# Each matmul of 512 moving columns made as two of 256, in the products with results by token, in a decoder layer on one core

## The chip, the core and the metric

The kernel runs on one core of one Trainium2 chip. The metric is the time of one execution on the device, in microseconds; the median of the timed runs counts. A profile of one execution shows what each engine did: PE is TensorE's matmul, PEld its load of a stationary tile, DVE is VectorE, ACT is ScalarE, POOL is GpSimd, SP is SyncE, which issues the DMAs.

## What is computed

One hybrid decoder layer for 256 tokens of 2048 features, in float32: a SwiGLU half-step, a mixer of two branches (MLA attention and HGRN2), and a second SwiGLU half-step, each with a norm ahead and one behind.

```python
D_MODEL, SEQ, D_FF, IN_COLS = 2048, 256, 5632, 13376

def swiglu(h, w_gate, w_up, w_down):
    return (jax.nn.silu(h @ w_gate) * (h @ w_up)) @ w_down
...
def token_mixer(h, positions, w_in, ...):
    proj = h @ w_in
    c_q, c_kv, k_rope, hq, hf, hi, hg, gate_a, gate_b = split_columns(proj)
    y_a = mla_branch(c_q, c_kv, k_rope, positions, ...)
    y_b = hgrn2_branch(hq, hf, hi, hg, lower_bound, ...)
    merged = jax.nn.sigmoid(gate_a) * y_a + jax.nn.sigmoid(gate_b) * y_b
    return merged @ w_out
...
        x = x + 0.5 * rmsnorm(swiglu(rmsnorm(x, ...), ...), ffn1_norm_post)
        x = x + rmsnorm(token_mixer(rmsnorm(x, ...), ...), mix_norm_post)
        x = x + 0.5 * rmsnorm(swiglu(rmsnorm(x, ...), ...), ffn2_norm_post)
```

Nearly all of the work is products of the 256 tokens with weight matrices, which are read once from memory.

## The kernel before

**Operands.** Every float32 operand of a large product is held as an exact sum of two parts of type float32r, `hi` and `lo`. A product is the sum of three: hi·hi, hi·lo and lo·hi. The activations stand transposed in SBUF as `[128 features, part, k-tile, 256 tokens]` (`h`, `after`, `h2` for the normed input of a stage; `at` for the SwiGLU's inner values; `mg` for the merged branches; `cqT`, `ckvT` for the two latents). Weights arrive by DMA on SP's queue in tiles `raw` of 128 x 1024 (512 KB, four buffers, line 83). ACT casts such a tile to its `hi` part `whi` (line 95), DVE subtracts to get `wlo` (line 96), with four buffers each. Where a tile has to be kept for later, both parts go into one tile `wpair` of a stage's own pool.

**Two kinds of product.** `gemm_t` (lines 111 to 115) holds weights as the stationary operand, 128 columns of them, and moves the tokens: the result is transposed, [column, token]. There `hi` weights move 512 columns (256 tokens in both parts) and `lo` weights 256. `gemm_n` holds the activations, 128 tokens at a time, as the stationary operand and moves the weights: the result is [token, column], one PSUM bank of 512 columns for each half of the tokens. It calls `_tok` for each k-tile and each half `tt` of the tokens; `_tok` makes the three matmuls of lines 126, 127 and 128 (hi·hi, hi·lo, lo·hi), the first two with the same stationary tile. A weight tile of 1024 holds two k-tiles of 512 columns, so it feeds twelve matmuls. A call with n=256 (the attention's values, `w_v`) has four k-tiles of 256 columns in a weight tile, and 24 matmuls.

**Where `gemm_n` is used.** With 512 columns: four products for the down projection of each half-step (stationary `at`, 44 k-tiles), the first gate and up columns of each half-step (`h`), the latents `c_q` and `c_kv`, the values and gates of the HGRN branch (`after`), the rotary part of the queries (`cqT`, four k-tiles) and four products for `w_out` (`mg`). With 256 columns: the eight products of `w_v` (`ckvT`, four k-tiles).

**Late halves.** At the end of a stage the last product (`closing`) lets the first half of the tokens finish its last `late` k-tiles before the second half starts them, so that the norm and residual of the first half run beside the second half's matmuls. The weights of those k-tiles are held, the first three tiles in `whi`/`wlo`, the others in `wpair`. The first products of the next stage do the same with all their k-tiles.

**Order.** Engines run their queues in order. The queues are filled by a scheduler in the order of the program; a block under `ahead()` is put ahead by 400 instructions (`AHEAD`), which is how a stage's closing chain (norm, transposes' results) gets in front of the weight casts.

Of the kernel before, what the change touches and what calls it, by code (L numbers as in the profile page):

```python
# [19 lines left out]
P = 128  # L20
# [16 lines left out]

# Where the next operand's transposes stand in program order, along the product that runs beside them (see gemm_n), and
# by how many instructions the rest of that operand's chain is put ahead; columns of the residual at a time.
AHEAD = 400  # L40
# [8 lines left out]
def _two_pi_parts():  # L49
    """2 pi as a sum of four 12-bit numbers and a rest."""  # L50
    parts, rest = [], TWO_PI
    for _ in range(4):
        step = 2.0 ** (np.floor(np.log2(rest)) - 11)
        c = np.floor(rest / step) * step
        parts.append(float(c))
        rest -= c
    parts.append(float(np.float32(rest)))
    return parts


class Ops:
    """Pools and the pieces that the stages share."""

# [15 lines left out]

# [1 line left out]
    def fetch(self, src):  # L81
# [17 lines left out]
    def gemm_t(self, w, act, kt):  # L99
        """256 weight columns, result transposed: a bank for 128 columns, [column, token] in two addends."""  # L100
        nc = self.nc
        ps = self.mm.tile([P, 2, 512], F32, name="mm")
        for g in range(kt // 4):
            hi, lo = self.load_w(w[g])
            for i in range(4):
                k = g * 4 + i
                for j in range(2):
                    c = slice(i * 256 + j * P, i * 256 + (j + 1) * P)
                    both = act(k)
                    if k == 0:  # L110
                        nc.tensor.matmul(ps[:, j], hi[:, c], both, start=True, stop=False)  # L111
                        nc.tensor.matmul(ps[:, j, 0:T], lo[:, c], both[:, 0], start=False, stop=False)  # L112
                    else:
                        nc.tensor.matmul(ps[:, j, 0:T], lo[:, c], both[:, 0], start=False, stop=False)  # L114
                        nc.tensor.matmul(ps[:, j], hi[:, c], both, start=False, stop=k == kt - 1)  # L115
        return ps

    def total(self, out, ps):
        """The sum of gemm_t's two addends."""
        self.nc.scalar.copy(out=out, in_=ps[:, :, T:512])  # L120
        self.nc.vector.tensor_tensor(out=out, in0=out, in1=ps[:, :, 0:T], op=ALU.add)

    def _tok(self, ps, hi, lo, act, k, kt, i, n, tt):
        nc = self.nc
        r, c, both, o = slice(tt * P, (tt + 1) * P), slice(i * n, (i + 1) * n), act(k), ps[tt][:, 0:n]
        nc.tensor.matmul(o, both[:, 0, r], hi[:, c], start=k == 0, stop=False)  # L126
        nc.tensor.matmul(o, both[:, 0, r], lo[:, c], start=False, stop=False)  # L127
        nc.tensor.matmul(o, both[:, 1, r], hi[:, c], start=False, stop=k == kt - 1)  # L128

    def gemm_n(self, w, act, kt, n=512, late=0, pool=None, own=0, hooks=()):  # L130
        """n weight columns, result [token, column], a bank for each half of the tokens.

        The first half of the tokens ends its last `late` k-tiles before the second half starts them. Their
        weights are in `pool`, but for the first `own` tiles. `hooks` are functions to call at points that run
        from -1 to 0 along the first half of the tokens, and from 0 to 1 along the second's last k-tiles."""
        kg = 1024 // n
# [29 lines left out]

# [1 line left out]
    def square_sum(self, acc, src):  # L168
# [3 lines left out]
    def rstd_of(self, ssq, n, width, half=False):  # L172
        """ssq [P, n] sums of squares -> 1 / sqrt(mean + eps), or half of it."""
        f = 4.0 if half else 1.0
# [19 lines left out]
    def transposed(self, src, act, c, tt):  # L194
        """split(transpose(src)) into the k-tiles 4c.. of act."""
        pt = self.tp.tile([P, 4, P], F32, name="tp")
# [9 lines left out]
    def prenorm(self, x, ssq, wname, act, tt, ws=None):  # L206
        """act = split(transpose(x * rstd * w)) for half of the tokens."""
        with self.ahead():
# [9 lines left out]
    def weighted(self, ps, c, z, wname):  # L218
        """z = y * w, a quarter of the columns."""
        w = self.bcast(wname, c)  # L220
        self.nc.vector.tensor_tensor(out=z[:, c * 512:(c + 1) * 512], in0=ps, in1=w, op=ALU.mult)

    def residual(self, x, z, rstd, done):
        """x += rstd * z, some of the columns at a time."""
        for c in range(D // RC):
# [4 lines left out]

    def closing(self, w, act, kt, late, own, pool, post, half, x_src, x_dst, nxt):
        """The last product of a stage, its norm, the residual, and the next stage's operand.

        Returns the hooks of the next product, which end the operand."""
        z = [pool.tile([P, D], F32, name=f"z{tt}") for tt in range(NT)]
# [32 lines left out]
def layer_kernel(ctx, tc, a, out):  # L268
# [9 lines left out]
    def ffn(n, act, fp, x_src, x_dst, nxt, hooks=()):  # L278
        at = [fp.tile([P, 2, 4, T], F32R, name="at", tag="s8", bufs=ops.slots) for _ in range(KF // 4)]
        wg, wu = a[f"ffn{n}_w_gate"], a[f"ffn{n}_w_up"]  # L280

        # the first columns by halves of the tokens
        pg = ops.gemm_n(a[f"ffn{n}_w_gate0"], act, KD, late=KD, pool=fp, own=4, hooks=hooks)
# [26 lines left out]

# [1 line left out]
    with fpool(1) as fp:  # L312
# [20 lines left out]

# [1 line left out]
    mix = ExitStack()  # L335
# [48 lines left out]

# [1 line left out]
    ops.slots = KF // 4  # L386
# [4 lines left out]
def rope_tables(ops, pool):  # L391
    """cos and sin of positions * inv_freq as [token, half of the tokens, HALF]."""
    nc, a = ops.nc, ops.a
# [15 lines left out]

    # whole turns off: their number in parts of ten bits, so that each product with a part of 2 pi is exact  # L410
    turns = pool.tile([P, n], F32, name="turns")
# [21 lines left out]
def mla(ops, mp, c_q, hm, h, oa, gate):  # L433
# [16 lines left out]
    def rope(dst, src, tt, n):  # L450
        """src [P, n, 64] -> dst, rotated."""
        s1, s2 = src[:, :, 0:HALF], src[:, :, HALF:ROPE]
# [16 lines left out]

    # k_rope: product transposed, back to [token, dim], rotated, transposed, for the even and the odd  # L470
    # head of a pair in its half of the partitions, with zeros in the other
    hi, lo = ops.load_w(a["w_krope"][0])
# [51 lines left out]
    def scores(pair, qn, kn, v):  # L524
        """The weights of a pair of heads, and what is left to do with them."""
        ws = []
# [44 lines left out]

    # a pair's projections, the weights of the pair before, and the output of that one later on
    later = []
# [25 lines left out]
def hgrn(ops, gp, h, ob, fill):  # L599
# [7 lines left out]

    # lower bound: first row of the softmax over the two rows of logits
    lg = gp.tile([P, 2, NH], F32, name="lg")
# [13 lines left out]
    def pair_in(pr, step):  # L623
        """q, f, k as [feature, half of the tokens, head, token]; the second half runs back in time."""
        tmp = lambda: gp.tile([P, 2, 2, P], F32, name="tmp", bufs=2)
# [27 lines left out]
    def values_in(g):  # L653
        """Values of four heads, [token, half of the tokens, head and feature]."""
        ps = ops.gemm_n(a["w_hi"][g], h, KD)
# [4 lines left out]
    def gates_in(g):  # L660
        """Their output gates, with the norm's weights."""
        ps = ops.gemm_n(a["w_hg"][g], h, KD)
# [10 lines left out]
    def scan(pr, q, f, k, four):  # L673
        """pre: products of f within blocks up to and with t; suf: products after s to the end of the block.

        Scores of pairs (s, t) in the two halves of a block of 2n tokens are k suf . q pre with blocks of n. In
        the second half of the tokens time runs back, so that there an earlier s has the place of a later
        one in the first half: one product gives both."""
        pre = f
# [6 lines left out]
        def part(t, n, early):  # L686
            """The earlier (or later) halves of the blocks of 2n: [P, half of the tokens, block, n]."""
            a0, a1 = (0, n) if early else (n, 0)
            return view(t, a0, [[256 + a1 - a0, 2], [2 * n, 128 // n], [1, n]])

        def ends(t, n, early):
            """The last element in time of those halves, over n columns."""
            a0, a1 = (n - 1, n) if early else (2 * n - 1, 0)
            return view(t, a0, [[256 + a1 - a0, 2], [2 * n, 128 // n], [0, n]])

        def halves(t, n, tt, early):
            """The same as part, of one half of the tokens: [P, block, n]."""
            off = n if early == bool(tt) else 0
# [91 lines left out]

    # a pair's products, the scores of the one before, and the output of the one before that
    later = []
# [30 lines left out]

# [1 line left out]
def _tiles(w, cols, group):  # L825
    """[K, C] -> [C / cols, K / (group * 128), 128, group * cols]"""
    k, c = w.shape
# [5 lines left out]
def _tokens(x):  # L833
    """Tokens in the kernel's order: the second half runs back in time."""
    return np.concatenate([x[:P], x[P:][::-1]])
# [63 lines left out]
```

## Time and profile before

| | |
|---|---|
| median of three timed runs | 2564.39 us (2564.30 to 2566.51) |
| profiled execution, first to last instruction (span) | 2564.2 us; no other time of it is listed, so 0.2 us lies between it and the median |
| PE busy | 2521.4 us, 98% |
| PEld busy (runs beside PE) | 2147.1 us |
| DVE, ACT, POOL busy | 1477.7, 1186.9, 181.1 us |
| granted TensorE clock, mean | 0.999 |
| moved from and to memory | 481 MB, 188 GB/s |
| under lines 126, 127, 128: matmuls of 512 columns | 1,296 each, 3,888 in all |
| under the same lines: matmuls of 256 columns (`w_v`) | 64 each, 192 in all |

In the profile's rows `L126 PE MATMUL mm<-whi,at 128*128 128x512` is a matmul of line 126 that writes `mm`, moves 512 columns of `whi` and has a stationary tile of `at` of 128 x 128. The duration of one matmul includes its way through the array; consecutive ones overlap, so that the time from start to start is less than the duration. In the timeline a row starts with the start in us from the start of the span and the duration in us.

### The profile page before, as it was taken

The numbers are of one execution on the slowest core, as the hardware profiler recorded it, in microseconds if no ns is written. First come the engines' busy times: TensorE is split into PE (matmuls) and PEld (weight loads), VectorE is DVE, ScalarE is ACT, GpSimd is POOL, SyncE is SP. The second block draws the span as 40 slices with busy tenths as digits, with TensorE's granted clock in tenths as the row PEclk, the third lists the DMA queues.
The fourth block names the chain that finished last, engine by engine and source line by source line (L and its number), as shares of the span: only waits on it lengthen the run. The fifth ranks groups of instructions, "written<-read, shape, count | busy, mean of one in ns | idle before, by whom it ended". The sixth has DMA issues, their size and how long they took to land.

```text
span 2564.2 us, 33907 instructions
## 1 busy us (share of the span) xinstructions
PE 2521.4 (98%) x13316; PEld 2147.1 (84%) x13316; DVE 1477.7 (58%) x1732; ACT 1186.9 (46%) x1552; POOL 181.1 (7%) x181
## 2 busy tenths in 40 slices
PE   8999999999999999999999999999999999999998
PEld 6888888888878898888888888888788888888887
DVE  5555555544466666556777776555655555554444
ACT  5444444434344556444444444444544444443433
POOL 0000000000000100111323231120000000000000
PEclk9999999999999999999999999999999999999999
DMA  7555555556686444555545444567755555555655
GB/s 255 174 188 189 188 183 190 188 188 199 201 271 188 162 140 148 188 181 181 165 163 169 161 157 158 188 205 242 231 175 188 187 186 188 189 189 188 197 195 184
DMA packets 137248, 481.13 MB, mean 188 GB/s; under 512 B 15616, under 2 KB 16000, under 8 KB 136320
## 3 DMA queue, kind: packets, MB, share of 16 engines
q1 hardware_dynamic: 137088, 478.97, 57.3%
q8 instruction: 104, 1.70, 0.3%
q14 instruction: 56, 0.46, 0.1%
HBM read 472.61 MB, written 6.29 MB: 187 GB/s over the span
## 4 chain that ended last, share of the span: by engine, by line
PE 93%; DVE 3%; POOL 1%; issue 1%; DMA 1%; ACT 1%; SPq 0%; POOLq 0%; DVEq 0%; ACTq 0%
PE mm L115 34%; PE mm L114 18%; PE mm L126 11%; PE mm L127 11%; PE mm L128 11%; PE mm L111 2%; PE mm L112 1%; POOL suf L706 1%; PE tp L198 0%; DVE sT L711 0%; PE sp L534 0%; PE sp L533 0%; DVE wlo L96 0%; PE sp L728 0%; PE tp L565 0%
## 5 line engine op out<-in xcount | busy, mean ns | idle before, releaser
L96 DVE TENSOR_TENSOR wlo<-raw,whi 128x1024 fp32r<-128x1024 f32 x826 | 1024.8, 1243 | 763.5 <-ACT whi L95 762.3
L95 ACT CAST whi<-raw 128x1024 fp32r<-128x1024 f32 x826 | 865.7, 1050 | 891.2 <-PE mm L115 425.3
L115 PE MATMUL mm<-h,whi 128*128 128x512 f32 x2400 | 846.0, 393 | 0.0
L114 PE MATMUL mm<-h,wlo 128*128 128x256 f32 x2400 | 678.1, 283 | 0.0
L115 PEld LDWEIGHTS mm<-h,whi 128*128 128x128 f32 x2400 | 450.7, 188 | 100.7
L114 PEld LDWEIGHTS mm<-h,wlo 128*128 128x128 f32 x2400 | 451.2, 188 | 3.8
L115 PE MATMUL mm<-after,whi 128*128 128x512 f32 x960 | 340.1, 394 | 0.0
L114 PE MATMUL mm<-after,wlo 128*128 128x256 f32 x960 | 273.1, 284 | 0.0
L127 PE MATMUL mm<-wlo,at 128*128 128x512 f32 x664 | 262.0, 395 | 0.0
L126 PE MATMUL mm<-whi,at 128*128 128x512 f32 x664 | 262.0, 395 | 0.0
L128 PE MATMUL mm<-whi,at 128*128 128x512 f32 x664 | 261.7, 395 | 0.0
L115 PEld LDWEIGHTS mm<-after,whi 128*128 128x128 f32 x960 | 180.4, 188 | 38.9
L114 PEld LDWEIGHTS mm<-after,wlo 128*128 128x128 f32 x960 | 180.6, 188 | 1.2
L126 PEld LDWEIGHTS mm<-whi,at 128*128 128x128 f32 x664 | 125.1, 188 | 29.2
L128 PEld LDWEIGHTS mm<-whi,at 128*128 128x128 f32 x664 | 125.1, 188 | 29.2
L127 PEld LDWEIGHTS mm<-wlo,at 128*128 128x128 f32 x664 | 125.1, 188 | 29.2
L178 POOL TENSOR_TENSOR rs<-ms,mhalf 128x1 f32<-128x1 f32 x16 | 9.7, 605 | 1633.3 <-DVE ms L176 1633.3
L126 PE MATMUL mm<-whi,after 128*128 128x512 f32 x304 | 120.9, 398 | 1.2 <-ACT after L164 1.2
L128 PE MATMUL mm<-whi,after 128*128 128x512 f32 x304 | 120.1, 395 | 0.0
L127 PE MATMUL mm<-wlo,after 128*128 128x512 f32 x304 | 120.0, 395 | 0.0
L115 PE MATMUL mm<-oa,whi 128*128 128x512 f32 x240 | 84.6, 393 | 0.0
L115 PE MATMUL mm<-ob,whi 128*128 128x512 f32 x240 | 84.6, 393 | 0.0
(276 smaller groups left out, 2860.9 us busy)
## 6 DMA issues: line engine op xcount, KB each, us to landing
raw<-in_ffn_w_gate SPq DMA_DIRECT2D x176, 512.0 KB, 4.3
raw<-in_ffn_w_up SPq DMA_DIRECT2D x176, 512.0 KB, 3.5
raw<-in_ffn_w_down SPq DMA_DIRECT2D x176, 512.0 KB, 4.3
raw<-in_w_ga SPq DMA_DIRECT2D x32, 512.0 KB, 3.4
raw<-in_mla_w_o SPq DMA_DIRECT2D x32, 512.0 KB, 3.6
raw<-in_w_hq SPq DMA_DIRECT2D x32, 512.0 KB, 3.6
raw<-in_w_hf SPq DMA_DIRECT2D x32, 512.0 KB, 3.5
raw<-in_w_hi SPq DMA_DIRECT2D x32, 512.0 KB, 3.5
```

Of the source, the lines that this page charges most:

```text
L95: nc.scalar.copy(out=hi, in_=raw)
L96: nc.vector.tensor_tensor(out=lo, in0=raw, in1=hi.bitcast(F32), op=ALU.subtract)
L111: nc.tensor.matmul(ps[:, j], hi[:, c], both, start=True, stop=False)
L112: nc.tensor.matmul(ps[:, j, 0:T], lo[:, c], both[:, 0], start=False, stop=False)
L114: nc.tensor.matmul(ps[:, j, 0:T], lo[:, c], both[:, 0], start=False, stop=False)
L115: nc.tensor.matmul(ps[:, j], hi[:, c], both, start=False, stop=k == kt - 1)
L126: nc.tensor.matmul(o, both[:, 0, r], hi[:, c], start=k == 0, stop=False)
L127: nc.tensor.matmul(o, both[:, 0, r], lo[:, c], start=False, stop=False)
L128: nc.tensor.matmul(o, both[:, 1, r], hi[:, c], start=False, stop=k == kt - 1)
L178: self.nc.gpsimd.tensor_tensor(out=r, in0=ms, in1=self.mhalf[:, 0:n], op=ALU.pow)
L706: G.tensor_tensor(out=part(suf, n, True), in0=part(suf, n, True), in1=ends(pre, n, False), op=ALU.mult)
```

## The change

In `_tok`, each matmul over n moving columns becomes one for every 256 of them, with the same stationary tile, into the two halves of the same PSUM bank. The very first matmul of an accumulation (k-tile 0, hi·hi), which clears the bank, stays whole. Calls with n=256 stay as they were. Comments and docstrings are dropped; nothing else differs in the source. From line 129 on, line numbers are four higher.

```diff
         r, c, both, o = slice(tt * P, (tt + 1) * P), slice(i * n, (i + 1) * n), act(k), ps[tt][:, 0:n]
-        nc.tensor.matmul(o, both[:, 0, r], hi[:, c], start=k == 0, stop=False)
-        nc.tensor.matmul(o, both[:, 0, r], lo[:, c], start=False, stop=False)
-        nc.tensor.matmul(o, both[:, 1, r], hi[:, c], start=False, stop=k == kt - 1)
+        for part, w in ((0, hi), (0, lo), (1, hi)):
+            if k == 0 and w is hi and part == 0:
+                nc.tensor.matmul(o, both[:, part, r], w[:, c], start=True, stop=False)
+                continue
+            for b in range(0, n, 256):
+                nc.tensor.matmul(o[:, b:b + 256], both[:, part, r], w[:, i * n + b:i * n + b + 256], start=False,
+                                 stop=k == kt - 1 and part == 1 and b + 256 == n)
```

On TensorE, at the start of the first down product, behind the last transposed product of the gate and up columns (`h`). Before:

```order
L115 MATMUL mm<-h_86,whi 128x512
L126 MATMUL mm<-whi,at 128x512
L127 MATMUL mm<-wlo,at 128x512
L128 MATMUL mm<-whi,at 128x512
L126 MATMUL mm<-whi,at 128x512
L127 MATMUL mm<-wlo,at 128x512
L128 MATMUL mm<-whi,at 128x512
L126 MATMUL mm<-whi,at 128x512
```

And now:

```order
L115 MATMUL mm<-h_86,whi 128x512
L128 MATMUL mm<-whi,at 128x512
L131 MATMUL mm<-wlo,at 128x256 x2
L131 MATMUL mm<-whi,at 128x256 x2
L128 MATMUL mm<-whi,at 128x512
L131 MATMUL mm<-wlo,at 128x256 x2
L131 MATMUL mm<-whi,at 128x256 x4
L131 MATMUL mm<-wlo,at 128x256 x2
```

The six matmuls of k-tile 0 (two halves of the tokens) become ten; from k-tile 1 on each matmul stands twice, and the order of the three products is kept.

The scheduler's lead of 400 instructions now spans fewer k-tiles, so a few neighbouring rows of ACT, DVE and SP change places. On ACT, around the third and the start of the fourth product of `w_out` (`ssq` rows are the squares of that product's result, which let its bank go). Before:

```order
L95 CAST whi<-raw 128x1024 x6
L95 CAST wpair<-raw 128x1024
L95 CAST whi<-raw 128x1024
L95 CAST wpair<-raw 128x1024
L170 ACTIVATE junk,ssq_14529<-mm 128x512
L95 CAST wpair<-raw 128x1024
L170 ACTIVATE junk,ssq_14530<-mm 128x512
L95 CAST wpair<-raw 128x1024 x2
```

And now:

```order
L95 CAST whi<-raw 128x1024 x5
L95 CAST wpair<-raw 128x1024
L95 CAST whi<-raw 128x1024
L95 CAST wpair<-raw 128x1024
L95 CAST whi<-raw 128x1024
L95 CAST wpair<-raw 128x1024
L174 ACTIVATE junk,ssq_16749<-mm 128x512
L95 CAST wpair<-raw 128x1024
L174 ACTIVATE junk,ssq_16750<-mm 128x512
L95 CAST wpair<-raw 128x1024
```

One more cast of held weights stands ahead of the first square.

## The prediction

> **What bounds the kernel now.** I read the page first (busy shares, chain, groups), then the stretches by engine, then the timeline of TensorE's rows. From the page:
>
> ```profile
> span 2564.2 us, 33907 instructions
> PE 2521.4 (98%) x13316; PEld 2147.1 (84%) x13316; DVE 1477.7 (58%) x1732; ACT 1186.9 (46%) x1552; POOL 181.1 (7%) x181
> PE 93%; DVE 3%; POOL 1%; issue 1%; DMA 1%; ACT 1%; SPq 0%; POOLq 0%; DVEq 0%; ACTq 0%
> PE mm L115 34%; PE mm L114 18%; PE mm L126 11%; PE mm L127 11%; PE mm L128 11%; PE mm L111 2%; PE mm L112 1%; POOL suf L706 1%; PE tp L198 0%; DVE sT L711 0%; PE sp L534 0%; PE sp L533 0%; DVE wlo L96 0%; PE sp L728 0%; PE tp L565 0%
> L96 DVE TENSOR_TENSOR wlo<-raw,whi 128x1024 fp32r<-128x1024 f32 x826 | 1024.8, 1243 | 763.5 <-ACT whi L95 762.3
> L95 ACT CAST whi<-raw 128x1024 fp32r<-128x1024 f32 x826 | 865.7, 1050 | 891.2 <-PE mm L115 425.3
> ```
>
> TensorE is busy for 98% of the span and is 93% of the chain that ended last. The three lines that the change rewrites, L126 to L128, are 11% each: a third of the chain. The engines that prepare weights are far from full: a tile of 1024 weight columns costs ACT 1.05 us and DVE 1.24 us and feeds twelve matmuls of 512 columns, which take 2.8 us (below). So whatever changes the time between the starts of these matmuls, which I call the pitch, moves the end of the program by the same amount.
>
> The mean of one matmul in the groups (395 ns) is no pitch: consecutive matmuls overlap, so I take starts from the timeline. In the down product of the first half-step, the first and the last of 57 matmuls in a row:
>
> ```profile
> 639.77 0.39 PE L127 MATMUL mm<-wlo,at 128*128 128x512 f32 x1
> ...
> 652.78 0.39 PE L126 MATMUL mm<-whi,at 128*128 128x512 f32 x1
> ```
>
> 56 steps in 13.01 us: 232.3 ns for 512 columns. The other two kinds of stretch under these lines are the output product of the mixer (first and last of 7), and weights held in the pool of their own, `wpair` (first and last of 16):
>
> ```profile
> 1774.62 0.39 PE L126 MATMUL mm<-whi,mg 128*128 128x512 f32 x1
> ...
> 1776.02 0.39 PE L126 MATMUL mm<-whi,mg 128*128 128x512 f32 x1
> 742.46 0.39 PE L128 MATMUL mm<-wpair,at 128*128 128x512 f32 x1
> ...
> 745.86 0.39 PE L128 MATMUL mm<-wpair,at 128*128 128x512 f32 x1
> ```
>
> 6 steps in 1.40 us, 233.3 ns; 15 steps in 3.40 us, 226.7 ns. The same instruction thus has two paces, 226.7 and some 232 to 233 ns, with nothing waiting in either.
>
> **The change part by part.** The built program has 13,060 matmul instructions before and 16,892 after. The 3,832 more are 3,832 of the 3,888 matmuls of 512 columns, each now two; the 56 that open an accumulation stay whole. The profile's line counts give the split by kind (three lines of each): 420 move `wpair`, 316 are whole-tile matmuls on `mg`, the remaining 3,096 are like the `at` row. Each new matmul brings a weight load of its own: the profile has as many loads as matmuls, and L126 and L127, which use one stationary tile after the other, each have theirs.
>
> The two costs to find are therefore the pitch of a matmul of 256 columns and whether its load hides. The product for the attention's values runs through the very same lines with 256 columns (n=256), on the same `whi` and `wlo` buffers. Its eight products are the nearest row in form:
>
> ```profile
> 897.62 0.36 PE L126 MATMUL mm<-whi,ckvT 128*128 128x256 f32 x1
> 897.83 0.28 PE L127 MATMUL mm<-wlo,ckvT 128*128 128x256 f32 x1
> 897.94 0.28 PE L128 MATMUL mm<-whi,ckvT 128*128 128x256 f32 x1
> 898.06 0.28 PE L126 MATMUL mm<-whi,ckvT 128*128 128x256 f32 x1
> 898.18 0.28 PE L127 MATMUL mm<-wlo,ckvT 128*128 128x256 f32 x1
> 898.30 0.28 PE L128 MATMUL mm<-whi,ckvT 128*128 128x256 f32 x1
> ...
> 900.23 0.28 PE L127 MATMUL mm<-wlo,ckvT 128*128 128x256 f32 x1
> 847.25 0.28 PE L126 MATMUL mm<-whi,ckvT 128*128 128x256 f32 x1
> 847.25 0.19 PEld L127 LDWEIGHTS mm<-wlo,ckvT 128*128 128x128 f32 x1
> 847.36 0.28 PE L127 MATMUL mm<-wlo,ckvT 128*128 128x256 f32 x1
> 847.37 0.19 PEld L128 LDWEIGHTS mm<-whi,ckvT 128*128 128x128 f32 x1
> ```
>
> After some uneven steps of 0.11 to 0.12 us, 17 steps take 1.93 us: 113.5 ns, so two halves take 227.0 ns. The last four rows show the loads (PEld): each starts with the matmul ahead of it and lasts 0.19 us, and the next matmul still starts 0.11 us later. Loads of consecutive matmuls overlap each other and the matmuls; the added 3,832 loads cost nothing by themselves at this pitch. The cover is the matmul ahead; without it a load of 0.19 us would stand alone.
>
> The Trainium skill has a rule against the change: its page "TensorE: Matmul & The Clock Gate", Part 3, section "The mechanism", says that a weight load overlaps matmuls in flight only when it targets another row group. All loads here fill all 128 rows, so by that rule 3,832 added loads of 0.19 us would be exposed, some 728 us; the trace's rows above contradict it, and I give it no chance.
>
> Two other rows bound the pitch from above. The product for the rotary key has 256 moving columns and stationary tiles of 64 columns (first and last of 15):
>
> ```profile
> 813.37 0.28 PE L477 MATMUL mm<-after,whi 128*64 128x256 f32 x1
> ...
> 815.01 0.28 PE L479 MATMUL mm<-after,wlo 128*64 128x256 f32 x1
> 300.02 0.40 PE L115 MATMUL mm<-h,whi 128*128 128x512 f32 x1
> 300.25 0.28 PE L114 MATMUL mm<-h,wlo 128*128 128x256 f32 x1
> 300.37 0.39 PE L115 MATMUL mm<-h,whi 128*128 128x512 f32 x1
> ```
>
> 14 steps in 1.64 us, 117 ns, or 234 for two. In the transposed products, where 256 and 512 columns alternate, the step behind a matmul of 256 is 0.12 us: 240 ns for two. So a half costs 113.5 to 120 ns, a pair 227 to 240, against 232.3 now. The lower end is a gain and the upper end a loss.
>
> I take the lower end. It is the same code line, operand kinds and buffers, its loads follow one another without a pause as they will after the change, and all its longer runs settle there within about five matmuls; the step of 0.12 us always has a matmul of 512 columns on one side. What speaks against it: the `wpair` stretch shows that operand placement alone moves the pitch by 6 ns, and `ckvT` lies elsewhere than `at`, `after` and `h`.
>
> The sum, against the profiled execution (2564.2 us; the median of the timed runs, 2564.39, lies 0.2 us from it):
> - 3,096 pairs at 232.3 - 227.0 = 5.3 ns less: 16.4 us.
> - 316 pairs on `mg` at 233.3 - 227.0 = 6.3 ns less: 2.0 us.
> - 420 pairs on `wpair`, 226.7 to 227.0: 0.1 us more.
> - Each of the 56 half-products starts with uneven steps, about 15 ns in all over five: 0.8 us more.
>
> Together 17.5 us less, all of it on the chain.
>
> What else moves: the built order of DVE, ACT and SP differs in a few neighbouring rows only, because the scheduler's lead of 400 instructions now spans fewer k-tiles. The largest shift is on ACT at the third quarter of the output product: one more cast of `wpair` stands ahead of the two squares.
>
> ```profile
> 1783.91 0.60 ACT L170 ACTIVATE junk<-mm 128x512 bf16<-128x512 f32 x1 [0.66 <-PE mm L128]
> 1784.99 1.05 ACT L95 CAST wpair<-raw 128x1024 fp32r<-128x1024 f32 x1 [0.39 <-DMA raw<-in_w_out]
> 1785.94 0.59 ACT L170 ACTIVATE junk<-mm 128x512 bf16<-128x512 f32 x1
> 1786.53 1.04 ACT L95 CAST wpair<-raw 128x1024 fp32r<-128x1024 f32 x1
> 1794.79 0.40 PE L126 MATMUL mm<-whi,mg 128*128 128x512 f32 x1
> ```
>
> The first square goes behind the cast that ends at 1786.04, 2.1 us later, the second behind one more cast. Their bank is next written at 1794.79, by the second half of the last product, some 7 us after: cost nothing. If that cover went, it would be at most these 2 us, once. DMA and the weight engines must deliver a tile every 2.72 instead of 2.79 us; DVE's 1.24 us is far below it. The instruction queue grows with the matmuls:
>
> ```profile
> q8 instruction: 104, 1.70, 0.3%
> ```
>
> 1.70 MB for 26,632 loads and matmuls is 64 bytes each; 7,664 more make 2.19 MB, 0.4% of the DMA engines' time. I cost it at nothing; the transfers are 30 more packets.
>
> **The rivals.**
>
> *No gain: the pair keeps the slow pace.* If 256 columns on these operands run at the rotary key's 117 ns, a pair takes 234 ns: 3,096 x 1.7 + 316 x 0.7 = 5.5 us more, and 3.1 us more still if the `wpair` pairs follow (420 x 7.3). That is 2564.2 to 2573, around 2569; it is as near to no change as to slower. For it: the operands there (`after` against `whi`) are the ones of most products, with the roles exchanged. Against it: stationary tiles of 64 columns are found nowhere in the changed products.
>
> The Trainium skill has this case as a rule: the same page, section "Back-to-back issue gap", gives a warm matmul a gap of N/2.4 plus 2.5 ns, a fixed cost for each. Worked out, an estimate from that page, 3,832 x 2.5 = 9.6 us more. Here the trace bears it out at the rotary key's pitch and not at the values', where two halves equal one whole to 0.3 ns.
>
> *Slower: each load takes something from the stream.* The excess over 226.7 ns may belong to the load, not to the columns: one load per 512 columns costs 5.6 ns on the `at` row, and a step of 0.12 us behind 256 columns in the transposed product is 6.6 ns over half of 226.7. With twice the loads it is paid twice. A pair then takes 238 to 240 ns: 3,832 x 5.7 to 7.7 = 22 to 30 us more, 2586 to 2594, if `wpair` follows only in part. It decides from a half's pitch of 116.2 ns on, half of 232.3. For it: the transposed products make the larger part of the evidence. Against it: the values' product pays two loads per 512 columns and no excess.
>
> *Fed too slowly.* Twice the instructions at 113 ns a pair of load and matmul over hundreds of matmuls may outrun TensorE's sequencer; the values' runs are only 24 long. Each step would then be over 116.2 ns too and join the case above.
>
> **How the numbers follow.** Changes under 0.2% (5.1 us) are about what a measurement of this kernel can't tell from none. Chances: the values' pitch throughout, 0.48, at 2564.4 - 17.5 = 2547 us, with its own range 2542 to 2553 (226 to 229 ns a pair); settled in part, pairs of 229 to 232 ns, 0.08, 2553 to 2564, of which half under 2559; the slow pace kept, 0.21, half each within 0.2% and slower; load paid twice, 0.20; too slow a feed, 0.03, slower. Faster 0.52, same 0.15, slower 0.33. The range reaches from 2542 to 2590: out are the upper half of the load case and the feed (0.13) and some 0.04 below.
>
> **What would show it.** In the profile after: twice the rows under the split line, 0.28 us each, starting 0.113 us apart in the down product, would show the pitch right; 0.117 or 0.12 the rivals. A down product's stretch of 100 us would hold some 880 matmuls (100 / 0.1135) instead of 430 (100 / 0.2323). Loads should still start with the matmul ahead. A gap on TensorE ended by "issue" would show the feed; idle time in front of L126's successor ended by ACT or DVE would show that a moved cast cost something. The prediction is wrong above all if the `ckvT` rows are a matter of where that tile lies.

## The result and the profile after

The changed kernel takes 2586.05 us (median; 2585.70 to 2590.15), the kernel before in the same series 2565.45 (2564.30 to 2568.03): a ratio of 1.0082 with a 95% interval of 1.0068 to 1.0096. It is 20.6 us slower where 17.5 us less were forecast. The page of the profile after, in the lines that answer to those of before:

```profile
span 2584.4 us, 41576 instructions
PE 2540.3 (98%) x17148; PEld 2336.7 (90%) x17148; DVE 1478.3 (57%) x1732; ACT 1186.5 (46%) x1552; POOL 186.0 (7%) x181
q8 instruction: 134, 2.20, 0.4%
PE 94%; DVE 2%; POOL 1%; issue 1%; DMA 1%; ACT 1%; SPq 0%; POOLq 0%; DVEq 0%; ACTq 0%
PE mm L131 34%; PE mm L115 34%; PE mm L114 18%; PE mm L111 2%; PE mm L112 1%; POOL suf L710 1%; PE mm L128 1%; PE tp L202 1%; DVE sT L715 0%; PE sp L538 0%; PE sp L537 0%; PE sp L732 0%; PE tp L569 0%; DVE x L231 0%; DMA wbc<-in_ffn_norm_pr
L96 DVE TENSOR_TENSOR wlo<-raw,whi 128x1024 fp32r<-128x1024 f32 x826 | 1025.3, 1244 | 766.2 <-ACT whi L95 764.0
L131 PE MATMUL mm<-whi,at 128*128 128x256 f32 x2624 | 419.7, 281 | 0.0
L131 PEld LDWEIGHTS mm<-whi,at 128*128 128x128 f32 x2624 | 357.6, 188 | 0.0
```

TensorE is as full as before and is 94% of the chain (93% before); DVE and ACT do the same work; the new line 131 has taken the place of the old three, with no idle time ahead of it (the last column of the two groups is 0.0). So the program is longer only because the same columns stream more slowly. The mean of a matmul (281 ns) says nothing of that, since matmuls overlap. The timeline of TensorE in the last part of the first down projection does; a row that ends in x4 stands for four matmuls in a row:

```profile
742.28 0.64 PE L131 MATMUL mm<-whi,at 128*128 128x256 f32 x4
742.76 0.40 PE L131 MATMUL mm<-wlo,at 128*128 128x256 f32 x2
742.99 0.64 PE L131 MATMUL mm<-whi,at 128*128 128x256 f32 x4
```

Six starts in 0.71 us are some 118 ns each. Counting over a longer stretch is finer. The view by stretches gives, for each one: its ends, its length, TensorE's busy time and the matmuls that touch it, the granted clock, and what the transfers did. About two of the matmuls counted only reach in from before the start, so I take off two. Before, 200 us of the down projection:

```profile
200.00:400.00 200.00, 200.00 (x1142) 1.00 0.58 187
530.00:730.00 200.00, 200.00 (x863) 1.00 0.64 207
```

and after, 30 us that hold halves alone:

```profile
726.00:756.00 30.00, 30.00 (x255) 1.00 0.67 222
```

Before, 861 matmuls in 200 us: 232.3 ns for 512 columns. After, 253 in 30 us: 118.6 ns for 256, 237.2 for two. (The stretch from 200 to 400 us is `gemm_t`, where widths of 256 and 512 alternate: 1,140 in 200 us, 350.9 ns a pair; it is needed below.) Where in the program the time went, by the intervals from each matmul's start to the next, summed over all rows of a kind: `whi` and `wlo` on `at`, `after` and `h` +13.1 us, `wpair` +6.4 us, on `mg` -0.1 us, `gemm_t` and all else within 0.3 us of before. The first matmul starts 0.7 us later than before (10.4 against 9.7 us).

### The profile page after: what moved, and what is told of

It is laid out like the page before. It is cut to its first block, busy times and chain, and to the rows that moved or that the text cites. A ratio compares the mean times of both kernels' runs of the same rounds, so it can differ in the third digit from the quotient of the medians.

```text
span 2584.4 us, 41576 instructions
## 1 busy us (share of the span) xinstructions
PE 2540.3 (98%) x17148; PEld 2336.7 (90%) x17148; DVE 1478.3 (57%) x1732; ACT 1186.5 (46%) x1552; POOL 186.0 (7%) x181
## 4 chain that ended last, share of the span: by engine, by line
PE 94%; DVE 2%; POOL 1%; issue 1%; DMA 1%; ACT 1%; SPq 0%; POOLq 0%; DVEq 0%; ACTq 0%
PE mm L131 34%; PE mm L115 34%; PE mm L114 18%; PE mm L111 2%; PE mm L112 1%; POOL suf L710 1%; PE mm L128 1%; PE tp L202 1%; DVE sT L715 0%; PE sp L538 0%; PE sp L537 0%; PE sp L732 0%; PE tp L569 0%; DVE x L231 0%; DMA wbc<-in_ffn_norm_pre 0%
## 5 line engine op out<-in xcount | busy, mean ns | idle before, releaser
L131 PE MATMUL mm<-whi,at 128*128 128x256 f32 x2624 | 419.7, 281 | 0.0
L131 PEld LDWEIGHTS mm<-whi,at 128*128 128x128 f32 x2624 | 357.6, 188 | 0.0
L131 PE MATMUL mm<-wlo,at 128*128 128x256 f32 x1328 | 265.6, 281 | 0.0
L131 PEld LDWEIGHTS mm<-wlo,at 128*128 128x128 f32 x1328 | 204.9, 188 | 0.8
L131 PE MATMUL mm<-whi,after 128*128 128x256 f32 x1176 | 189.9, 282 | 0.0
L131 PEld LDWEIGHTS mm<-whi,after 128*128 128x128 f32 x1176 | 160.9, 188 | 0.0
L131 PE MATMUL mm<-wlo,after 128*128 128x256 f32 x608 | 121.6, 281 | 0.0
L131 PEld LDWEIGHTS mm<-wlo,after 128*128 128x128 f32 x608 | 94.7, 188 | 1.0
L120 ACT COPY m<-mm 128x512 f32<-128x512 f32 x56 | 32.9, 587 | 97.1 <-PE mm L115 97.1
```

The costliest lines, as they stand in the source:

```text
L131: nc.tensor.matmul(o[:, b:b + 256], both[:, part, r], w[:, i * n + b:i * n + b + 256], start=False, stop=k == kt - 1 and part == 1 and b + ...
```

## The experiments

**The theory.** In the built program every buffer of `whi` and `wlo` starts at 160 modulo 256 bytes in its partition, `at`, `after`, `h` and `wpair` at 32, `mg` and `ckvT` at 224. I write `whi` on `at` for a matmul that moves `whi` and has `at` as its stationary tile, and call the start of the moving tile minus that of the stationary one, modulo 256 bytes, the place. Sorted by it, the pitches of the two kernels fall into classes: 226.7 (512 columns) and 120 ns (256) at place 0 (`wpair` on `at`), 232.3 and 118.65 at place 128 (`whi` on `at`), 233.3 and 113 to 118 at place 192 (`whi` on `mg`, on `ckvT`). The theory: the place sets what a matmul loses to the weight load beside it. Rivals: a fixed cost of each matmul; the other engines; the repetition of a stationary tile.

**Moving the weights.** In the kernel before (512 columns) and in the changed one (256), pads shift `raw`, `whi` and `wlo` against all other tiles; the second pad keeps the later pools on their places modulo 512:

```diff
         self.small = ctx.enter_context(tc.tile_pool(name="small", bufs=3))
+        for pool, n in ((self.wp, 128), (self.small, 384)):
+            if n:
+                self.nc.gpsimd.memset(pool.tile([P, n // 4], F32, name="pad", bufs=1), 0.0)
```

Labels give the width and the shift in bytes. Expected of 128 bytes on the kernel before:

> The kernel before (matmuls of 512 columns), with a pad of 128 bytes ahead of the pool that holds whi and wlo, and one of 384 bytes behind it, so that only raw, whi and wlo move, by 128 bytes in each partition, against at, after, h, mg, cqT and act; two memsets at the start are all that is added. Theory (placement): each matmul loses time to the weight load that runs beside it, by where its moving tile lies against that load's stationary tile, modulo 256 bytes. With the shift whi lies to at, after and h as wpair lies to at in the kernel before, so their pitch falls from 232.3 to 226.7 ns: 3,096 x -5.6 = -17.4 us; mg by about -4 ns x 316 = -1.3 us; the pair of gemm_t may fall from 350.8 towards 340 ns, at most 4,224 x -10.8 = -46 us. Together 2500 to 2547 us, against 2565. Rival (a fixed cost of each matmul, whatever the addresses): no change, 2563 to 2568 us, whi,at at 232.3 ns. Rival (the vector and scalar engines' work, or transfers, hold the stream up): no change either, since nothing of theirs moves.

Measured: 2550.47 us (ratio 0.9939, interval 0.9924 to 0.9954). Its stretches in `gemm_t` and in the down projection:

```profile
200.00:400.00 200.00, 200.00 (x1136) 1.00 0.56 187
530.00:730.00 200.00, 200.00 (x884) 1.00 0.64 212
```

882 in 200 us are 226.8 ns: the theory's number; a fixed cost of each matmul, or the other engines, would have left 232.3. The pads alone take 15 us off. `gemm_t` went the other way than expected, 1,134 matmuls or 352.7 ns a pair, so the time is 3.5 us above the range. The same pads on the changed kernel:

> The changed kernel (two matmuls of 256 columns) with the same pads: raw, whi and wlo moved by 128 bytes. Theory (placement): whi now lies to at as wpair does, and the halves of wpair,at went at 120 ns each in the changed kernel, so the halves of whi,at go from 118.65 to 120 ns: 3,096 x 2 x 1.35 = +8 us, mg +1 us, and gemm_t gains what it gains in the unsplit kernel with the same pads. So the split costs about 3,096 x (240 - 226.7) = +41 us and some 3 us more against that one, where it cost 20.6 us at the first placement. Rival (fixed cost of a matmul): 2586 us as the changed kernel without pads, halves at 118.65 ns.

Measured 2598.84 us (ratio 1.0126, interval 1.0111 to 1.0142):

```profile
726.00:756.00 30.00, 30.00 (x252) 1.00 0.71 242
```

250 in 30 us, 120.0 ns, as expected. The split now costs 48.4 us: at the place that is best for whole matmuls, halves are at their worst. A shift of 64 bytes:

> The kernel before with pads of 64 and 448 bytes: raw, whi and wlo moved by 64 bytes. Theory (placement): whi lies to at as it lay to mg, so 233.3 ns instead of 232.3 (3,096 x +1.0 = +3 us); whi to mg as wpair to at, 226.7 instead of 233.3 (316 x -6.6 = -2 us); gemm_t's pair as wpair to mg, about 347 instead of 350.8 ns (at most -17 us). 2549 to 2569 us. Rival (fixed cost): no change.

> The changed kernel with the pads of 64 and 448 bytes. Theory (placement): whi's halves lie to at as they lay to mg, between 113.3 and 117.8 ns (mean 116.5), instead of 118.65: 3,096 x 2 x -2.15 = -13 us if the mean holds, -33 us at 113.3; mg's halves 120 instead of 116.5 (+2 us); gemm_t 0 to -17 us. The split then costs about nothing against its unsplit sibling, or gains up to 20 us. Rival (fixed cost): 2586 us.

Measured 2567.93 us (1.0003, 0.9993 to 1.0012) and 2575.60 us (1.0038, 1.0027 to 1.0049). Down projection at 512 columns, then at 256:

```profile
530.00:730.00 200.00, 200.00 (x859) 1.00 0.62 207
```

```profile
726.00:756.00 30.00, 30.00 (x257) 1.00 0.70 229
```

857 in 200 us, 233.4 ns, and 255 in 30 us, 117.6 ns (a mean of 116.6 over all halves of `whi` and `wlo` on `at`): both the class of place 192. The split costs 7.7 us by the medians, where about nothing or a gain was expected. The two profiled executions lie 12.2 us apart (2562.41, the fastest of ten, and 2574.56); by the intervals between starts the split brings +5.6 us at `wpair` and +4.2 at `mg`, while `after` gains 2.8, `h` gains 1.3 and `at` stays even. Another +5.1 us lies in `gemm_t`, which the split does not touch: at this shift the time scatters from run to run. This unsplit kernel also answers the sentence with which the prediction ended. The rows of `ckvT`, from which its pitch was taken, here:

```profile
896.91 0.28 PE L129 MATMUL mm<-whi,ckvT 128*128 128x256 f32 x1
...
899.30 0.28 PE L131 MATMUL mm<-whi,ckvT 128*128 128x256 f32 x1
```

20 steps in 2.39 us, 119.5 ns instead of 113.5, on the same line with the same shapes. The place is not all that counts, though. The changed kernel leaves the products on `ckvT`, their widths and their place as they were. Five of its eight still settle at 113.5 ns as all eight did before, but three do not; in one of them, from its second matmul to its last:

```profile
920.95 0.28 PE L128 MATMUL mm<-whi,ckvT 128*128 128x256 f32 x1
...
923.31 0.28 PE L131 MATMUL mm<-whi,ckvT 128*128 128x256 f32 x1
```

20 steps in 2.36 us are 118.0 ns. The last shift of the grid, and a control that moves the weights and the later pools together:

> The kernel before with pads of 192 and 320 bytes: raw, whi and wlo moved by 192 bytes. Theory (placement): whi lies to at as wpair to mg in the kernel before, 229 ns instead of 232.3 (3,096 x -3.3 = -10 us), whi to mg as whi to at before (232.3 instead of 233.3); the pair of gemm_t between the 348.7 and 353.2 ns that the other two shifts gave, -9 to +10 us. 2546 to 2566 us. Rival (fixed cost): no change.

> The changed kernel with the pads of 192 and 320 bytes. Theory (placement): whi's halves lie to at as wpair's to mg, 117.8 ns instead of 118.65 (6,192 x -0.85 = -5 us), mg's 118.65 instead of 116.5 (+1.4 us), gemm_t -9 to +10 us: 2573 to 2593 us, and about +20 us against the unsplit kernel with the same pads (2 x 117.8 - 229 = 6.6 ns, 3,096 times). Rival (fixed cost): 2586 us.

> The kernel before with one pad of 128 bytes ahead of raw, whi and wlo and none behind: the weight tiles move by 128 bytes, and with them every pool that is taken after theirs (at, after, h, act, wpair), so that whi lies to at as in the kernel before; only mg, which is taken from the other end, stays. Theory (the place of the moving tile relative to the stationary tile counts): 232.3 ns for whi,at and 350.8 ns for a pair of gemm_t as before, 2562 to 2568 us. Rival (the address of whi itself counts, or the pad does something else): 226.7 ns and about 2551 us, as with whi alone moved by 128 bytes.

Measured 2564.21 us (0.9995, 0.9986 to 1.0005), 2585.93 (1.0081, 1.0065 to 1.0098) and 2564.75 (0.9996, 0.9987 to 1.0006). Down projections, in this order:

```profile
530.00:730.00 200.00, 200.00 (x875) 1.00 0.62 209
```

```profile
726.00:756.00 30.00, 30.00 (x256) 1.00 0.68 231
```

```profile
530.00:730.00 200.00, 200.00 (x863) 1.00 0.61 207
```

229.1 and 118.1 ns are the class of place 64 (`wpair` on `mg` before); what the unsplit kernel gains with that (10 us on `at` and `after`) it gives back in `gemm_t` (+7.6 us), so its time does not show it. In the control 861 matmuls take 200 us, 232.3 ns as before, though `whi` has moved by the same 128 bytes that gave 226.8 alone: the place relative to the stationary tile counts, not the address.

| place of `whi` on `at` | 512 columns, ns | 256 columns, ns (from 726 to 756 us) | unsplit, us | split, us | cost of the split |
|---|---|---|---|---|---|
| 128 (as given) | 232.3 | 118.6 | 2565.45 | 2586.05 | 20.6 |
| 192 (shift 64) | 233.4 | 117.6 | 2567.93 | 2575.60 | 7.7 |
| 0 (shift 128) | 226.8 | 120.0 | 2550.47 | 2598.84 | 48.4 |
| 64 (shift 192) | 229.1 | 118.1 | 2564.21 | 2585.93 | 21.7 |

Over all halves of `whi` and `wlo` on `at` the means are 118.7, 116.6, 120.0 and 116.7 ns, in the order of the table. At the shifts of 64 and 192 bytes the halves change their pace within the down projection, as the products on `ckvT` do. With 192 bytes, 40 us and the next 40:

```profile
600.00:640.00 40.00, 40.00 (x355) 1.00 0.55 191
640.00:680.00 40.00, 40.00 (x340) 1.00 0.60 204
```

353 and 338 matmuls are 113.3 and 118.3 ns.

**Is it each load?** If every load cost its share, a part of the split would cost a part of the 20.6 us. First the product with `wlo` alone, then the two with `whi` alone (in the first of these kernels the flags that open and close an accumulation go with the whole products):

```diff
         for part, w in ((0, hi), (0, lo), (1, hi)):
-            if k == 0 and w is hi and part == 0:
+            if w is hi:                            # the other kernel: if w is lo or (k == 0 and part == 0):
```

> One part of the change alone: of the three products the one with wlo is made as two matmuls of 256 columns (1,296 of the 3,888), the two with whi stay whole; no pads. If the cost comes with each added load: a third of the added time, 1,032 x (2 x 118.65 - 232.3) = +5.2 us at at, after and h, 140 x (240 - 226.7) = +1.9 us at wpair, 105 x about 0 at mg: 2572 us, 2570 to 2575. Rival (the cost comes with the repetition of a stationary tile, or with something that needs all three halves in a row): no change, 2565 us, or far from a third.

> The other part of the change alone: the two products with whi are made as halves (2,536 of 3,832), the one with wlo stays whole; no pads. The part with wlo alone gave +1.4 us. If the parts add up: 2565.5 + 20.6 - 1.4 = 2585 us. If each load costs the same: two thirds of +20.6 us, 2579 us. If the loss depends on the sequence of wide and narrow matmuls: neither, nearer to no change, 2565 to 2575 us.

Measured 2567.23 us (1.0007, 0.9998 to 1.0015) and 2568.92 us (1.0013, 1.0004 to 1.0023): +1.4 and +3.5 us. Stretches of the first and of the second:

```profile
720.00:750.00 30.00, 30.00 (x174) 1.00 0.74 245
```

```profile
720.00:750.00 30.00, 30.00 (x217) 1.00 0.68 231
```

172 and 215 in 30 us. The three products of a k-tile are four and five matmuls here and take 698 ns in both, against 3 x 232.3 = 697 unsplit and 6 x 118.6 = 712 with all three split. So the loss on these tiles is no fixed price of a load: one or two more loads in three products cost nothing, three cost 15 ns. My theory falls in that form; the sequence of widths matters beside the place. At place 0 it is otherwise: by the intervals between starts, `wpair` pays +2.2 us with one of the three products split, +4.3 with two and +6.4 with all, close to a third of the cost for each. The third kernel keeps all six halves in another order, the halves of the columns outermost, so that two halves of one product never meet:

```diff
-        for part, w in ((0, hi), (0, lo), (1, hi)):
...
-            for b in range(0, n, 256):
+        for b in range(0, n, 256):
+            for part, w in ((0, hi), (0, lo), (1, hi)):
```

> The changed kernel with the halves of the columns outermost: the three products on columns 0 to 255, then the three on 256 to 511, so that of the six matmuls no two that are halves of one product stand next to each other; no pads. If the cost were that of one stationary tile used for two matmuls in a row: most of the +20.6 us goes, about 2570 us. If each added load costs the same, in whatever order: 2586 us (2581 to 2591). If the order sets how the loads meet the streams, as the split of wlo alone suggests, anything between 2565 and 2600 us with halves at a pitch other than 118.65 ns.

Measured 2587.16 us (1.0086, 1.0071 to 1.0101), with the count of the changed kernel:

```profile
726.00:756.00 30.00, 30.00 (x255) 1.00 0.68 228
```

A matmul that repeats the stationary tile of the one before is now every third, as in the unsplit kernel, where it was four of six in the changed one; the count has not moved, so this repetition is not the cause. The time is the one that was expected if each added load cost the same, which the two kernels above speak against.

**Narrower matmuls.** Four matmuls of 128 columns for each of 512:

> The changed kernel with four matmuls of 128 columns in place of two of 256 (no pads). If each load adds one step of some 6 ns to the stream whatever its columns: 56.7 + 6 = 63 ns each, 252 ns for 512 columns instead of 237.3, 3,832 x +15 = +57 us, 2640 us. If the loads themselves bound it, at the 109 ns from start to start that matmuls of 128 columns have in the transposes (xn): 4 x 109 = 436 ns, 3,832 x +199 = +760 us, some 3350 us.

Measured 3692.12 us (two runs, ratio 1.4390, interval 1.4361 to 1.4419). Two stretches of down projections:

```profile
700.00:900.00 200.00, 200.00 (x1790) 1.00 0.31 106
1000.00:1200.00 200.00, 200.00 (x939) 0.50 0.25 86
```

1,788 in 200 us are 111.9 ns, nowhere near half of the 113.3 that 256 columns take without loss (half of 226.7). For the loads (PEld) the first stretch reads:

```profile
700.00:900.00 200.00, 199.83 (x1788) 1.00 0.31 106
```

They follow one another without a gap. That a load of 128 columns bounds each matmul fits this but is not shown, since no run has matmuls without their loads; if it does, the loads of halves are hidden with almost nothing to spare. Two stretches of some 215 and 230 us, the second one above among them, ran at a granted clock of 0.50 and 213 ns for each matmul. At 111.9 ns they would have been some 210 us shorter, an estimate: that is most of the 340 us beyond the expected 3350.

**Other places, and the best kernel.** Shifts between the multiples of 64, unsplit:

> The kernel before with pads of 96 and 416 bytes, for a placement between two that were measured. Theory (placement): whi,at between the 233.3 ns of the shift by 64 bytes and the 226.7 of that by 128; gemm_t's pair between 340 ns, which two matmuls without a lost step would take, and the 353 that was its worst: 2505 to 2570 us; if nothing between the multiples of 64 differs, one of the two neighbours' times, 2567 or 2550 us.

> The kernel before with pads of 160 and 352 bytes. Theory (placement): whi,at between 226.7 ns (shift by 128 bytes) and 229 (by 192); gemm_t's pair between 340 and 353 ns: 2500 to 2566 us; like a neighbour, 2550 or 2564 us, if nothing between the multiples of 64 differs.

> The kernel before with pads of 32 and 480 bytes. Theory (placement): whi,at between 232.3 ns (no shift) and 233.3 (by 64 bytes); gemm_t's pair between 340 and 353 ns: 2520 to 2570 us; 2565 or 2567 us, as its neighbours, if nothing between the multiples of 64 differs.

Measured 2553.87 us (0.9954, 0.9941 to 0.9968), 2571.80 (1.0017, 1.0002 to 1.0032) and 2568.15 (1.0010, 1.0001 to 1.0019). The shift of 160 bytes is 5.8 us above its range. Between multiples of 64 the pitches differ again, and two lie above both of their neighbours: with 160 bytes `whi` on `at` takes some 233.5 ns (856 in 200 us; 226.8 and 229.1 beside it), with 32 bytes some 234.4 (853; 232.3 and 233.4 beside it). With 96 bytes whole matmuls are slow too (857, 233.4 ns), but `gemm_t` has its best place:

```profile
200.00:400.00 200.00, 200.00 (x1154) 1.00 0.55 190
530.00:730.00 200.00, 200.00 (x859) 1.00 0.60 205
```

1,152 there are 347.2 ns a pair. The kernel that joins both bests takes these pads and moves `at` and `wpair` to the weights' place:

```diff
     with fpool(1) as fp:
+        G.memset(fp.tile([P, 56], F32, name="pad"), 0.0)
...
     with fpool(2) as fp:
+        G.memset(fp.tile([P, 56], F32, name="pad"), 0.0)
```

> The kernel before with the pads of 96 and 416 bytes, which gave gemm_t's pair 346.6 ns and whi,at 233.4, and a pad of 224 bytes at the head of the two ffn pools, so that at and wpair there lie at the same place modulo 256 bytes as whi. Theory (placement): whi,at at 226.7 ns as in the kernel with whi moved by 128 bytes, though it is at that moves here (1,992 x -6.7 = -13.3 us); wpair with h and after, moved apart, 226.7 to 233.4 (240 x +6.7 = +1.6 us); gemm_t stays at 346.6. 2553.9 - 11.7 = 2542 us, faster than all measured so far. Rival (the place of whi itself counts): 2554 us.

Measured 2541.68 us (0.9911, 0.9894 to 0.9927), 0.3 us from the forecast:

```profile
200.00:400.00 200.00, 200.00 (x1155) 1.00 0.56 190
530.00:730.00 200.00, 200.00 (x884) 1.00 0.64 213
```

`gemm_t` has kept its 346.9 ns a pair, and `whi` on `at` is at 226.8 ns again, this time because `at` moved. This kernel has whole matmuls of 512 columns and four pads, and beats both kernels of the case: it is 23.7 us faster than the one before.

## Why the prediction was wrong, point by point

- **The step that failed** is "I take the lower end": the pitch of a half was taken from the `ckvT` rows, 113.5 ns, as the row nearest in line, shape and buffers. It is 118.6 ns at `at`. What those rows had of their own was the place of `ckvT`, which the prediction named as the thing that would make it wrong; a shift of the weight tiles by 64 bytes, nothing else, took the same rows to 119.5 ns. Nor was 113.5 ns safe at that place: three of the eight products on `ckvT` themselves ran at 118 ns after the change, and halves on `at` moved to the same place took 116.6 ns in the mean. Two rows that bounded it from above (117 and 120 ns) were the better guides, and the paces of 226.7 and 232.3 ns for one and the same instruction were a sign that placement outweighs the code line.
- **The terms.** 3,096 pairs were to gain 16.4 us and lost 13.1. The 316 on `mg`, at the place of `ckvT`, were to gain 2.0 and came out even: their halves took 116.5 ns in the mean. The 420 on `wpair` were to cost 0.1 us and cost 6.4: best for whole matmuls (226.7 ns), this place is the worst for halves (120 ns). The prediction's "two halves equal one whole to 0.3 ns" set halves at place 192 against wholes at place 0; at place 0 two halves take 240.0 ns and a whole 226.8.
- **The rivals.** "Each load takes something from the stream" gave 2586 to 2594 us with a chance of 0.20, and 2586.05 was measured. That it met the number is luck in part: it priced each pair at 5.7 to 7.7 ns, and the runs have 4.2 in the mean on `at`, `after` and `h`, nothing on `mg` and 15 on `wpair`. The stated range, 2542 to 2590, holds the measured time only through its share of this rival; the forecast, and the chance of 0.52 for faster, pointed the other way. Its reason holds in part only: the loss follows the place of the stationary tile, which the load reads, but `lo_only` and `hi_only` show no fixed price of a load. "The slow pace kept" had the right kind of row and too small a price: 117 ns where 118.6 to 120 were found outside `mg`.
- **The Trainium skill**, page "TensorE: Matmul & The Clock Gate", has two rules that bear on this. Section "Back-to-back issue gap" has a formula, for a matmul that it calls isolated, in which no place of a tile enters; it would give the same cost wherever tiles lie, an estimate of 9.6 us; the runs have 7.7 to 48.4 us by place, so the measurement decides against it. Part 2, section "Step-by-step: what each phase is for", says that loading the next weights takes no read bandwidth from the running matmul, since the two have ports of their own; here the place of the stationary tile relative to the moving one changed the pitch of 512 columns from 226.8 to 233.4 ns, so in these runs the two are not independent in time, by whatever path.
- **What was right.** A third of the chain and 3,832 more matmuls and loads; no idle time on TensorE behind the moved casts; the instruction queue at 134 packets, 2.20 MB (2.19 worked out) and 0.4%; the loads hidden behind the matmul ahead (a load and a matmul every 111.9 ns in `q128`, under the 113.3 ns of a half without loss), which also leaves no feeding limit here; DVE and ACT unchanged. That what the pitch costs lands in the end time held in every run: in each profile 18 to 20 us of the span lie outside the intervals between matmul starts, whatever the pitch.
- **What stays open.** Why the loss of a place depends on the widths in the sequence, and why halves at places 192 and 64 have two paces (some 113.4 and 118 ns), even in one program, was not settled; nor was what makes the time scatter at some shifts. That load and stream meet in the same part of the memory is only argued: no run here had a matmul without its load.

## What to carry to other kernels

Take the price of a new shape from several rows that differ in their tiles, not from the one nearest in code: where the same instruction has two paces in one trace, find what separates them before choosing. On a TensorE-bound kernel, try where operands lie before how they are cut: pads of some hundred bytes took 15 and 24 us off here, and no cut into halves gained at any of the four places tried. Price an edit with matmul starts counted over a long stretch, since mean durations hide the pitch.

## What the runs showed of the hardware that was not expected

- The pitch of a 512-column float32r matmul is 226.7 to some 234 ns, and that of two halves 227 to 240 ns, and pads alone move them by changing the place of the moving against the stationary tile. A shift of 32 bytes already changes it (232.3 to some 234.4 ns for 512 columns). The best of the places for whole matmuls (226.8 ns) is the worst for halves (120.0). At some places halves have two paces in one program.
- At some places the time itself scatters more: ten runs with a shift of 160 bytes lay between 2557.49 and 2576.12 us, ten with 64 bytes between 2562.41 and 2571.53, while twenty-seven of the kernel before lay between 2564.41 and 2567.68.
- Under matmuls of 128 columns the granted clock fell to 0.50 for some 215 and 230 us (1000 to 1200 us: TensorE busy throughout, 213 ns for each); what sets it off wasn't tried.
